# Differential attention heads: outputs normed into one kept tile and transposed together, first softmax left unnormalised

## The chip, the cores and the metric

The kernel runs on one core of a Trainium2 chip. The metric is device time in microseconds (us) of one execution, the median of three runs. A profiled execution gives the trace; its own time stands beside its span below.

## What is computed

Two blocks in sequence on 512 tokens of width 1024. The first block has two hybrid layers, each with 4 differential, 8 stick-breaking and 8 forgetting attention heads, an output projection and norms; the second block has a recurrent branch, windowed attention and a feed-forward part. The change touches only the differential heads of the two hybrid layers:

```python
def diff_attention(q, k, v, lam, lambda_init, sub_gain):
    ...
        s = jnp.einsum('bhcqd,bhckd->bhcqk', q[:, :, :, q0:q1], k[:, :, :, :q1]).astype(jnp.float32) * scale
        allowed = chunk_id[:q1][None, :] <= chunk_id[q0:q1][:, None]
        p = jax.nn.softmax(jnp.where(allowed, s, -jnp.inf), axis=-1)
        w = p[:, :, 0] - lam * p[:, :, 1]
        outs.append(jnp.einsum('bhqk,bhkd->bhqd', w, v[:, :, :q1].astype(jnp.float32)))
    o = jnp.concatenate(outs, axis=2)
    return rms_norm(o, sub_gain) * (1.0 - lambda_init)
```

Two softmaxes per head (`p[:, :, 0]`, `p[:, :, 1]`) are combined into one weight matrix `w`, multiplied with the values, and each output row of 128 is divided by its root mean square (with 1e-6 added to the mean square).

## The kernel before

All matrix products with weights are three TensorE passes over a high and a low part of each operand (`mm3`), so TensorE has most of the work. A layer is a stream of projections, chunk by chunk, into which the attention of the heads is woven. `Pipe` (line 316) holds the stages of attention steps with lags: a differential head has four query blocks (steps i = 0 to 3, of key width 128, 256, 384 and 512), each step has the stages `a`, `b_`, `c`, `d`, due 0, 3, 5 and 8 ticks after its start, two ticks to a step. In a tick the due stages are issued, the latest stage first but `a` last, and then `Filler` issues projection matmuls up to a share of its total. Differential heads are n = 0 to 3, pair heads (stick-breaking, forgetting) n = 4 to 11. Heads 0 and 1 are given 3 chunks of projections, the later ones 3.97.

A differential step before the change (line 695):

- `a`: scores of the two softmaxes on TensorE into two PSUM banks; per softmax VectorE masks a corner (L704) and finds the row maximum (L706), ScalarE takes the exponential and sums the row (L709), VectorE inverts the sum (L711). VectorE then multiplies the second inverse by minus lambda (L715), scales the first exponential by its inverse (L716) and adds the second one times its factor (L717, called the merge here).
- `b_`: TensorE transposes the merged weights by 128-blocks into a bank (L143), and VectorE or ScalarE in turn copies them out (L511 on VectorE, L513 on ScalarE).
- `c`: TensorE multiplies them with the values into a bank; ScalarE squares and sums (L730); `rstd_of` makes mean and power, a [128, 1] VectorE operation (L357) and a GpSimd power (L361); VectorE scales the output into one of two small tiles (L732).
- `d`: TensorE transposes that tile into a quarter of a bank that the head keeps from i = 0 to i = 3; at i = 3 VectorE multiplies with gain and gate (L741), and `split` makes high and low parts (L267 on ScalarE, L268 on GpSimd).

Beside it, `rope` rotates q and k of the next head: shuffle (L520) on VectorE, a product on GpSimd (L522), a product (L523) and a sum (L524) on VectorE, then splits (L618 on ScalarE, L619 on VectorE). Weights are split by L219 (ScalarE) and L233 (VectorE and GpSimd), the gate is L631 and L632.

A scheduler sets the order on VectorE, ScalarE and GpSimd and which buffer a tile gets; TensorE keeps program order (`tc.keep_in_program_order`). Buffers: 8 PSUM banks, 6 tiles of tag `wT`, 24 [128, 1] tiles of tag `st`.

## Time and profile before

| | |
|---|---|
| median of 3 runs | 1808.55 us (1807.75 to 1809.88) |
| profiled execution: its own time, its span | 1806.02 us, 1804.2 us |
| TensorE busy | 1760.4 us, 98% of the span |
| VectorE busy | 1125.7 us, 62% |
| ScalarE busy | 765.3 us, 42% |
| GpSimd busy | 646.0 us, 36% |
| mean granted clock of TensorE | 0.994 |

The span is 1.8 us shorter than the execution's own time. Busy time of TensorE includes time at a lower granted clock, since a slower matmul is still busy. The differential heads lie at about 60 to 206 us (first layer) and 500 to 640 us (second layer). All rows name engines as PE (TensorE), PEld (its weight loads), DVE (VectorE), ACT (ScalarE), POOL (GpSimd).

### The profile page before, as it was taken

To read this page: it belongs to the slowest core of one execution; us is meant where nothing else is said; L and a number is where in the kernel's file an instruction comes from. 1 tells how busy PE (TensorE), PEld (TensorE's weight loads), DVE (VectorE), ACT (ScalarE), POOL (GpSimd) and SP (SyncE) were. 2 spreads that over 40 slices of the span, in tenths; PEclk is the share of its full clock that TensorE was granted. 3 is DMA by queue.
4 is the path that set the end of the run, shared out by engine and by line. 5 is a ranking of instruction groups with operands and counts; after the bars stand their busy time and mean duration, and the time that the engine had idled before them with its cause. 6 is when DMAs were issued, how large, how long until landed. Compare 5 with 4: busy or idle time off the path is not lost.

```text
span 1804.2 us, 26056 instructions
## 1 busy us (share of the span) xinstructions
PE 1760.4 (98%) x9774; PEld 1516.4 (84%) x9774; DVE 1125.7 (62%) x2450; ACT 765.3 (42%) x1461; POOL 646.0 (36%) x534
## 2 busy tenths in 40 slices
PE   9989999999999999999999999999999999999998
PEld 8778887888978888888899888788788888888898
DVE  5788889775588899876583678886423632222122
ACT  4445444443445544444433433777423432322221
POOL 3332221122333222122253545355545344444331
PEclk9999999999999999999999999999999999999999
DMA  5312222312321312322223232222333233333321
GB/s 199 92 54 82 66 66 94 106 60 82 121 70 53 94 60 71 112 78 93 66 94 106 82 90 87 88 70 100 111 96 109 94 95 103 96 94 99 100 97 67
DMA packets 51696, 162.12 MB, mean 90 GB/s; under 512 B 8482, under 2 KB 10050, under 8 KB 51571
## 3 DMA queue, kind: packets, MB, share of 16 engines
q1 hardware_dynamic: 51570, 160.46, 28.1%
q8 instruction: 77, 1.26, 0.3%
q14 instruction: 49, 0.39, 0.1%
HBM read 158.28 MB, written 2.16 MB: 89 GB/s over the span
## 4 chain that ended last, share of the span: by engine, by line
PE 81%; DVE 10%; issue 3%; ACT 2%; POOL 2%; DMA 1%; SPq 0%; POOLq 0%; DVEq 0%; ACTq 0%
PE ps L126 78%; PE ps L143 3%; DVE wl L233 2%; POOL e L522 1%; DVE e L763 1%; DMA raw<-in_wu_dram 1%; DVE e L520 1%; DVE st L706 1%; POOL st L361 1%; DVE yT L523 0%; ACT wh L219 0%; POOL wl L233 0%; DMA x<-in_x_dram 0%; DVE klow L619 0%; DVE e L764 0%
## 5 line engine op out<-in xcount | busy, mean ns | idle before, releaser
L233 POOL TENSOR_TENSOR wl<-raw,wh 128x368 fp32r<-128x368 f32 (+5 forms) x262 | 359.3, 1373 | 634.6 <-ACT wh L219 587.5
L126 PE MATMUL ps<-hTH,wh 128*128 128x512 f32 (+1 forms) x1336 | 531.8, 398 | 1.4 <-DVE sm L1135 1.4
L126 PE MATMUL ps<-hTL,wh 128*128 128x512 f32 (+1 forms) x1336 | 521.8, 391 | 0.0
L126 PE MATMUL ps<-hTH,wl 128*128 128x512 f32 (+1 forms) x1336 | 521.8, 391 | 0.0
L219 ACT CAST wh<-raw 128x1024 fp32r<-128x1024 f32 (+2 forms) x263 | 269.1, 1026 | 403.2 <-PE ps L126 219.5
L233 DVE TENSOR_TENSOR wl<-raw,wh 128x656 fp32r<-128x656 f32 (+6 forms) x261 | 256.1, 982 | 283.7 <-ACT wh L219 282.0
L126 PEld LDWEIGHTS ps<-hTH,wl 128*128 128x128 f32 x1336 | 252.4, 189 | 53.8
L126 PEld LDWEIGHTS ps<-hTH,wh 128*128 128x128 f32 x1336 | 252.7, 189 | 49.4 <-issue 1.9
L126 PEld LDWEIGHTS ps<-hTL,wh 128*128 128x128 f32 x1336 | 252.9, 189 | 46.8
L126 PE MATMUL ps<-wh,yT 128*128 128x512 f32 (+1 forms) x544 | 161.5, 369 | 0.0
L126 PEld LDWEIGHTS ps<-wh,yT 128*128 128x128 f32 x544 | 98.5, 189 | 16.0 <-issue 0.3
L126 PE MATMUL ps<-wh,hTH 128*128 128x256 f32 (+2 forms) x496 | 106.5, 303 | 3.2 <-ACT hTH L383 1.7
L361 POOL TENSOR_TENSOR st<-st,half_neg 128x1 f32<-128x1 f32 x64 | 37.6, 587 | 198.3 <-DVE st L359 116.6
L126 PE MATMUL ps<-wl,hTH 128*128 128x256 f32 (+2 forms) x496 | 106.8, 300 | 0.5 <-POOL wl L233 0.5
L126 PE MATMUL ps<-wh,hTL 128*128 128x256 f32 (+2 forms) x496 | 105.7, 300 | 0.0
L126 PE MATMUL ps<-wl,yT 128*128 128x512 f32 (+1 forms) x272 | 99.4, 365 | 0.0
L126 PEld LDWEIGHTS ps<-wh,hTH 128*128 128x128 f32 x496 | 84.9, 208 | 5.0 <-ACT hTH L383 2.1
L143 PE MATMUL ps<-ident,e 128*128 128x128 f32 x460 | 71.1, 276 | 15.1 <-DVE e L764 5.8
L126 PEld LDWEIGHTS ps<-wl,hTH 128*128 128x128 f32 x496 | 84.6, 208 | 0.9 <-POOL wl L233 0.7
L126 PEld LDWEIGHTS ps<-wh,hTL 128*128 128x128 f32 x496 | 84.2, 208 | 0.1
L126 PE MATMUL ps<-y,y 128*128 128x128 f32 (+2 forms) x240 | 69.8, 322 | 6.1 <-ACT e L709 5.0
L143 PEld LDWEIGHTS ps<-ident,e 128*128 128x128 f32 x460 | 53.5, 141 | 26.0 <-issue 11.1
(331 smaller groups left out, 2851.2 us busy)
## 6 DMA issues: line engine op xcount, KB each, us to landing
raw<-in_wu_dram SPq DMA_DIRECT2D x263, 512.0 KB, 3.5
bc<-cum SPq DMA_DIRECT2D x16, 256.0 KB, 5.4
raw<-in_wu_dram SPq DMA_DIRECT2D x10, 256.0 KB, 2.5
yT<-back SPq DMA_DIRECT2D x8, 256.0 KB, 4.3
raw<-in_wu_dram SPq DMA_DIRECT2D x4, 396.0 KB, 3.0
x<-in_x_dram SPq DMA_DIRECT2D x3, 512.0 KB, 8.0
out_dram<-x SPq DMA_DIRECT2D x3, 512.0 KB, 2.7
gain<-in_post_norm_dram SPq DMA_DIRECT2D x2, 512.0 KB, 4.8
```

The costliest lines, as they stand in the source:

```text
L126: tc.keep_in_program_order(nc.tensor.matmul(*args, **kw))
L143: tc.keep_in_program_order(nc.tensor.transpose(dst, src, ident))
L219: order(copy(h[:, : r.shape[1]], r))
L233: order(e.tensor_tensor(lo[:, d], r[:, d], h[:, d].bitcast(F32), op=ALU.subtract))
L361: order(G.tensor_tensor(r, m, half_neg, op=ALU.pow))
L520: V.stream_shuffle(sh[:n], t[:n], mask)
L522: G.tensor_tensor(shv, shv, sinT, op=ALU.mult)
L706: V.tensor_reduce(mx, ps[:, :w], axis=AX.X, op=ALU.max, negate=True)
L763: V.tensor_tensor_scan(rev, rev, rev, 1.0, ALU.mult, ALU.bypass)
```

## The change

The first softmax is left unnormalised: the merged matrix is exp0 - lam * (sum0/sum1) * exp1, that is, w times the row sum of the first exponential. The norm that follows divides the scale out again; so that the 1e-6 has the right weight, it is multiplied by that row sum squared (`eps`) and added to the mean square. The normed outputs of the four steps go to the four quarters of one `wT` tile that the head keeps, and stage `d` does nothing until i = 3, where it takes a bank, transposes all four quarters into it and goes on as before.

```diff
             def a():
-                es, rs = [], []
+                es, dens = [], []
...
                     ACT.activation(e[:, :w], ps[:, :w], AF.Exp, bias=mx, accum_out=den)
-                    r = stat()
-                    V.reciprocal(r, den)
                     es.append(e)
-                    rs.append(r)
-                r1 = stat()
-                V.tensor_tensor(r1, rs[1], neglam, op=ALU.mult)
-                V.tensor_scalar(es[0][:, :w], es[0][:, :w], rs[0], None, ALU.mult)
+                    dens.append(den)
+                r1, eps = stat(), stat()
+                V.reciprocal(r1, dens[1])
+                V.scalar_tensor_tensor(r1, r1, neglam, dens[0], ALU.mult, ALU.mult)
                 V.scalar_tensor_tensor(es[0][:, :w], es[1][:, :w], r1, es[0][:, :w], ALU.mult, ALU.add)
-                loc["w"] = es[0]
+                V.scalar_tensor_tensor(eps, dens[0], EPS, dens[0], ALU.mult, ALU.mult)
+                loc["w"], loc["eps"] = es[0], eps
...
-                o1 = small(P, 2, "o1")
+                if i == 0:
+                    s["o1"] = [oall[:, P * q : P * (q + 1)] for oall in (work("wT"),) for q in range(4)]
+                o1 = s["o1"][i]
                 ssq = stat()
                 ACT.activation(o1, o[:, :P], AF.Square, accum_out=ssq)
-                r = rstd_of(ssq, P)
+                m, r = stat(), stat()
+                V.scalar_tensor_tensor(m, ssq, 1.0 / P, loc["eps"], ALU.mult, ALU.add)
+                G.tensor_tensor(r, m, half_neg, op=ALU.pow)
                 V.tensor_scalar(o1, o[:, :P], r, None, ALU.mult)
-                loc["o1"] = o1
 
             def d():
-                if i == 0:
-                    s["yps"] = bank()
-                transpose(s["yps"][:, P * i : P * (i + 1)], loc["o1"])
-                if i == 3:
-                    sg = s["sg"]
-                    V.scalar_tensor_tensor(sg, s["yps"], subl, sg, ALU.mult, ALU.mult)
-                    chunks[n] = split(sg, "yT")
+                if i < 3:
+                    return
+                yps = bank()
+                for q, o1 in enumerate(s["o1"]):
+                    transpose(yps[:, P * q : P * (q + 1)], o1)
+                sg = s["sg"]
+                V.scalar_tensor_tensor(sg, yps, subl, sg, ALU.mult, ALU.mult)
+                chunks[n] = split(sg, "yT")
```

In the changed kernel the lines of a step are: inverse L713, factor L714, merge L715, eps L716, square L731, mean L733, power L734, scaling of the output L735, gain and gate L744. Per step VectorE has one wide operation less (L716 of before) and as many [128, 1] operations as before (four). TensorE's order is the same but for the transposes of `d`; the DMA queue's order is the same.

The scheduler sets VectorE's and ScalarE's orders anew over all differential heads. VectorE, first layer, head 1, step 0 (128 wide): from the first row maximum to the merge. `ps_910`, `ps_911` (before) and `ps_899`, `ps_900` (changed) are the two score banks; `e_939` and `e_926` are the shuffled k or q of the next head.

Before:

```order
L706 TENSOR_REDUCE st_917<-ps_910 128x1
L732 TENSOR_SCALAR sm_885<-ps_882,st_890 128x128
L711 RECIPROCAL st_922<-st_920 128x1
L706 TENSOR_REDUCE st_925<-ps_911 128x1
L716 TENSOR_SCALAR e_919<-e_919,st_922 128x128
L511 COPY wT_982<-ps_977 128x512
L711 RECIPROCAL st_930<-st_928 128x1
L520 STREAM_SHUFFLE e_939<-e_937 128x512
L715 TENSOR_TENSOR st_932<-st_930,sm_477 128x1
L523 TENSOR_TENSOR e_937<-e_937,rope_464 128x512
L717 SCALAR_TENSOR_TENSOR e_919<-e_927,st_932,e_919 128x128
```

Changed:

```order
L706 TENSOR_REDUCE st_906<-ps_899 128x1
L704 MEMSET ps_900 64x64
L233 TENSOR_TENSOR wl_1234<-raw_1231,wh_1233 128x656
L706 TENSOR_REDUCE st_912<-ps_900 128x1
L713 RECIPROCAL st_917<-st_915 128x1
L716 SCALAR_TENSOR_TENSOR st_918<-st_909 128x1
L714 SCALAR_TENSOR_TENSOR st_917<-st_917,sm_477,st_909 128x1
L715 SCALAR_TENSOR_TENSOR e_908<-e_914,st_917,e_908 128x128
L520 STREAM_SHUFFLE e_926<-e_924 128x512
```

The inverse of the second sum now stands directly behind the second row maximum, with no other VectorE work between them; before, the wide scaling L716 and a PSUM copy stood there. The merge moved ahead of the shuffle.

ScalarE, first layer, head 0, steps 1 and 2: the copy (L513, 128x256) of step 1's transposed weights.

Before:

```order
L709 ACTIVATE e_797,st_798<-ps_781,st_795 128x384
L513 COPY wT_828<-ps_825 128x256
L631 ACTIVATE sg_830<-ps_760 128x512
L730 ACTIVATE sm_817,st_818<-ps_815 128x128
L709 ACTIVATE e_856,st_857<-ps_847,st_854 128x512
```

Changed:

```order
L709 ACTIVATE e_785,st_786<-ps_776,st_783 128x384
L631 ACTIVATE sg_824<-ps_756 128x512
L219 CAST wh_1115<-raw_1113 128x1024
L709 ACTIVATE e_791,st_792<-ps_777,st_789 128x384
L731 ACTIVATE wT_811,st_812<-ps_809 128x128
L513 COPY wT_822<-ps_819 128x256
L709 ACTIVATE e_850,st_851<-ps_841,st_848 128x512
```

The copy now stands behind the gate, a weight cast, step 2's second exponential and step 0's square; before, it stood directly behind step 2's second exponential, ahead of the gate and the square.

TensorE, first layer, stage `d` of head 0 at i = 3, just ahead of the scores of head 1, step 3.

Before:

```order
L143 MATMUL ps_908<-ident_84,sm_1056 128x128
L126 MATMUL ps_1154<-y_739,y_643 128x512
L126 MATMUL ps_1154<-klow_91,y_643 128x512
L126 MATMUL ps_1155<-y_739,y_643 128x512
L126 MATMUL ps_1155<-klow_91,y_643 128x512
```

Changed:

```order
L143 MATMUL ps_1127<-ident_84,wT_811 128x128 x4
L126 MATMUL ps_1137<-y_735,y_643 128x512
L126 MATMUL ps_1137<-klow_91,y_643 128x512
L126 MATMUL ps_1138<-y_735,y_643 128x512
L126 MATMUL ps_1138<-klow_91,y_643 128x512
```

Three transposes came here from earlier places. As placed in the built programs, the second score bank here (`ps_1155`, `ps_1138`) is in both kernels the bank of the first scores of the step before it (head 1, step 2), which that step's first exponential frees. The next value projection's second bank follows the output of a step in the kernel before (freed by L732), and an older tile, the transposed weights of head 2, step 0, in the changed one.

## Rows read from the trace of the kernel before

**Rows 1.** Busy us by stretch: PE, PEld, DVE, ACT, POOL; granted clock; DMA share, GB/s.
```profile
60.00:140.00 80.00, 71.90 (x380) 59.85 (x379) 70.08 (x179) 39.79 (x101) 27.66 (x26) 0.98 0.20 61
...
500.00:580.00 80.00, 73.41 (x393) 61.95 (x392) 67.59 (x182) 39.33 (x101) 27.89 (x26) 0.96 0.23 70
```

**Rows 2.** TensorE's timeline: start, us, instruction, [idle before <- what ended it].
```profile
104.03 0.33 PE L143 MATMUL ps<-ident,sm 128*128 128x128 f32 x1 [0.83 <-DVE sm L732]
...
107.25 0.50 PE L126 MATMUL ps<-y,y 128*128 128x512 f32 x1 [2.43 <-ACT e L709]
...
134.12 0.74 PE L126 MATMUL ps<-wh,hTH 128*128 128x256 f32 x4 [1.23 <-DVE sm L732]
...
519.63 0.52 PE L143 MATMUL ps<-ident,e 128*128 128x128 f32 x3 [2.54 <-DVE st L357]
...
544.22 0.50 PE L126 MATMUL ps<-y,y 128*128 128x512 f32 x1 [1.80 <-ACT e L709]
...
571.02 0.74 PE L126 MATMUL ps<-wh,hTH 128*128 128x256 f32 x4 [0.29 <-DVE sm L732]
```

**Rows 3.** VectorE's waits, 60 to 140 us: the two longest.
```profile
DVE sm L732 <- POOL st L361: 4.0, 6, 1.7
DVE st L711 <- ACT e L709: 2.0, 7, 0.4
```

**Rows 4.** VectorE's waits, 500 to 580 us: three of them.
```profile
DVE sm L732 <- POOL st L361: 5.2, 8, 1.7
DVE st L711 <- ACT e L709: 2.1, 4, 0.8
...
DVE ps L704 <- PE ps L126: 1.3, 1, 1.3
```

**Rows 5.** Line 716 alone (wide scaling) by stretch: DVE busy (count), clock, DMA.
```profile
60.00:140.00 80.00, 4.66 (x11) 0.98 0.20 61
...
500.00:580.00 80.00, 4.64 (x11) 0.96 0.23 70
```

**Rows 6.** Instructions of lines 715 and 359: ns min/median/max.
```profile
L715 DVE TENSOR_TENSOR st<-st,sm x32: 139/158/750, 70.0 to 608.9; 128x1 f32<-128x1 f32 x32
...
L359 DVE SCALAR_TENSOR_TENSOR st<-st,st,per_d x32: 210/219/533, 6.1 to 1798.9; 128x1 f32<-128x1 f32 x32
```

**Rows 7.** Groups by shape, 60 to 140 us: busy us, mean ns | idle before.
```profile
L511 DVE COPY wT<-ps 128x384 f32<-128x384 f32 x2 | 1.1, 548 | 0.0
...
L709 ACT ACTIVATION_READ_ACCUMULATOR e<-ps,st 128x1 f32 x22 | 4.2, 193 | 0.0
...
L709 ACT ACTIVATE e<-ps,st 128x256 f32<-128x256 f32 x6 | 2.8, 475 | 4.8 <-DVE st L706 4.8
L709 ACT ACTIVATE e<-ps,st 128x512 f32<-128x512 f32 x4 | 2.7, 687 | 4.7 <-DVE st L706 4.7
L709 ACT ACTIVATE e<-ps,st 128x128 f32<-128x128 f32 x6 | 2.2, 368 | 8.4 <-DVE st L706 8.4
```

**Rows 8.** Busy us in 2 us stretches, as rows 1: granted clock third from last.
```profile
108.00:110.00 2.00, 2.00 (x6) 1.50 (x6) 1.94 (x7) 1.76 (x6) 1.40 (x2) 0.50 0.00 0
110.00:112.00 2.00, 2.00 (x10) 1.65 (x9) 1.84 (x3) 0.60 (x1) 1.44 (x2) 0.66 0.33 61
...
546.00:548.00 2.00, 2.00 (x6) 1.61 (x5) 1.97 (x9) 1.33 (x5) 1.53 (x2) 0.50 0.00 0
```

**Rows 9.** VectorE's timeline after the differential heads: a wait for TensorE.
```profile
209.40 0.54 DVE L756 TENSOR_TENSOR ps<-ps,masks 128x128 f32<-128x128 f32 x2 [1.59 <-PE ps L126]
```

**Rows 10.** VectorE's timeline: two merges and two rotary products.
```profile
70.15 0.35 DVE L717 SCALAR_TENSOR_TENSOR e<-e,st,e 128x128 f32<-128x128 f32 x1
...
74.80 0.69 DVE L523 TENSOR_TENSOR e<-e,rope 128x512 f32<-128x512 f32 x1
...
92.50 1.38 DVE L717 SCALAR_TENSOR_TENSOR e<-e,st,e 128x128 f32<-128x128 f32 x1
...
130.69 1.78 DVE L523 TENSOR_TENSOR e<-e,rope 128x512 f32<-128x512 f32 x1
```

## The prediction

> **What bounds the kernel now.** I read the page first: TensorE is busy for 98% of the span, so only its idle time and its time at a low clock can be won. Then the busy time by stretch. While heads 0 and 1 run, TensorE is idle for 80 - 71.90 = 8.1 us in the first layer and 80 - 73.41 = 6.6 us in the second, and VectorE is busy for 70.1 and 67.6 of the 80 us [rows 1]. Together that is 14.7 us of idle time in the two stretches that the change can reach. In the waits view VectorE waits for GpSimd's power (4.0 and 5.2 us) and for the exponentials (2.0 and 2.1 us), and for TensorE only once, 1.3 us in the second layer [rows 3, 4]. So in these stretches VectorE's chain sets the pace: what comes off it comes off TensorE's idle time, up to the 14.7 us. The timeline of TensorE shows where it stands still [rows 2]: for merged weights (2.54 us at 519.63), for the normed output at i = 3 (0.83 us at 104.03), for a score bank that the last step's exponential must free (2.43 and 1.80 us at 107.25 and 544.22), and for a bank of the value projection (1.23 and 0.29 us at 134.12 and 571.02). After the longer ones the clock falls to its lower level: the granted clock is 0.50 and 0.66 in the two stretches of 2 us after 108 us, and 0.50 again at 546 us [rows 8]. The first costs (1 - 0.50) x 2 + (1 - 0.66) x 2 = 1.7 us.
>
> A gain here lasts. At 209.40 us VectorE waits 1.59 us for TensorE [rows 9]: from there VectorE has time over, and TensorE's earlier arrival is passed on.
>
> **Part by part.** *The wide scaling goes.* L716 takes 4.66 and 4.64 us in the two stretches, 11 runs each [rows 5]: 9.3 us off VectorE. The other 10 runs lie in heads 2 and 3, where TensorE has no idle time to win, and count nothing.
>
> *The [128, 1] operations stay four to a step, but three become scalar_tensor_tensor.* L715 takes 158 ns as a tensor_tensor, a scalar_tensor_tensor of this size 219 ns [rows 6]. That bounds the cost between 0 (the two that take constants run like L715) and 3 x 0.06 us a step. I take 0.10, since only the factor reads a scalar from memory as L359 does: 22 steps, 2.2 us.
>
> *VectorE has less to do while the second exponential runs.* In the order of head 1, step 0, the inverse now stands directly behind the second row maximum. It waits for an exponential and its read: 0.37 + 0.19 = 0.56 us at width 128, 0.67 at 256, 0.88 at 512 [rows 7]; 384 has no row here, and 0.78 lies between. Where a PSUM copy covers it (0.55 us at 384) 0.33 is left. Of the 11 steps of the stretch in the first layer six are bare or thinly covered: 2 x 0.56 + 0.67 + 0.5 + 2 x 0.4 = 3.1 us. In the second layer five are: 1.1 + 0.88 + 0.56 + 0.67 + 0.5 = 3.7 us (the 1.1 where the first exponential is late too). The sum is 6.8 us, against 4.1 us of such waits now [rows 3, 4]: 2.7 us more. Ends: 0, if the queues drift so that the exponential is done, and 6.8.
>
> *Waits for the power.* Between mean (L733) and scaling of the output (L735) less work stands than before: the gate product (L632) no longer stands there in the first layer. Going through the 11 steps of the first layer with about 0.7 us to cover, I find 3.6 us uncovered where the same count for the order before gives 2.5. I take 1.0 us a layer, 2.0 in all; ends 0 and 9.2, the waits there now [rows 3, 4], once more.
>
> *Transposes and banks.* There are 32 transposes of normed outputs before and after; three of four move to the last step of the head, so they cost TensorE nothing. The wait at 104.03 is for the fourth output and stays [rows 2]. The head's bank is free between i = 0 and i = 3, but taken just ahead of the scores at which TensorE waits at 107.25 and 544.22, and the second of these score banks still is that of the step before: the 2.43 and 1.80 us go only as far as VectorE gets faster. The value projection's bank comes from an older tile now: 1.23 + 0.29 = 1.5 us go [rows 2].
>
> *One kept `wT` tile.* In differential heads one or two of six are in use, so this costs nothing; a pair head needs all six, but takes the last two three ticks after the last differential head has given its tile back.
>
> *The clock.* If the stops at 107 and 544 us get shorter, the low clock behind them may stay away: 0 to 2 x 1.7 = 3.4 us, the second taken like the first [rows 8]. I take half, 1.7.
>
> **Sum.** VectorE's chain: 9.3 - 2.2 - 2.7 - 2.0 = 2.4 us; bank 1.5; clock 1.7; together 5.6 us. The profiled execution's own 1806.02 us becomes 1800.4. The median of the runs is 2.5 us above it, so for a median I take 1808.55 - 5.6 = 1803.0 us.
>
> **The rivals.**
>
> *Full relief.* The scheduler covers the new waits with weight splits, and only the dearer small operations are paid: 9.3 - 2.2 + 1.5 + 3.4 = 12.0 us, 1796.5 us. For it speaks that both exponentials can now follow the scores without an inverse between them, so banks come free earlier. Against it, the bare places in the order. Its limit is all idle time and both low stretches, 14.7 + 3.4 = 18.1 us.
>
> *The waits take it all.* If the wait for the exponential counts in full (6.8 instead of 2.7), VectorE's chain is 9.3 - 2.2 - 6.8 - 2.0 = -1.7 us, and without help from the clock 1.5 us of bank are left: about 1808.7, no change.
>
> *GpSimd blocks the merge.* In five places (head 0, step 1, and head 1, step 1, of both layers, and head 1, step 0, of the second) the merge now stands between the shuffle and the rotary product, as GpSimd starts its own product. A merge took 0.35 us at 70.15 and 1.38 us, at the same width, at 92.50 beside GpSimd's product; a rotary product took 0.69 us at 74.80 and 1.78 us at 130.69, behind a merge placed so [rows 10]. At five places 1.78 - 0.69 = 1.1 us each, 5.5 us: 1803.0 + 5.5 = 1808.5, no change. It decides only if GpSimd gets in between. The Trainium skill states it as a rule (SBUF — State Buffer, "SBUF: two separate sides"): a VectorE instruction with two SBUF inputs and a GpSimd instruction exclude each other, and the later one waits for the whole of the first. The two rows agree with that rule.
>
> *Slower: the copy of step 1 comes late.* ScalarE's copy of step 1's transposed weights (second layer: VectorE's) now stands behind the gate, a weight cast and the next step's second exponential. TensorE's value product needs it and would stop for up to a cast, a gate and an exponential more, some 2.5 us, at a place where it now has 1 to 2 us to wait anyway. If that costs 1.3 us a layer, a stop of this length also brings the low clock (1.7 us), and the stop at 107 us remains: 2 x 3.0 - 1.5 = 4.5 us, 1813.0 us. It decides from the point where the copy lands after the merged weights of step 2. Against it: the second exponential follows the first sooner now.
>
> **How the numbers follow.** About 0.2% (3.6 us) is what a measurement of this kernel can tell from no change: faster is below 1804.9, slower above 1812.2. The forecast has 0.45, of which 0.40 is below 1804.9; full relief 0.17; no change by the waits 0.21; by GpSimd 0.07; slower 0.10. So faster 0.40 + 0.17 = 0.57, same 0.05 + 0.21 + 0.07 = 0.33, slower 0.10. The range goes from a little below full relief, 1796.0, to 1809.5, a little above no change; it leaves out the slower case and half of what lies beyond full relief. The forecast's own range is 1800 to 1806.
>
> **What would show it.** Right: L716's wide operation is gone, TensorE's idle time from 60 to 140 and from 500 to 580 us sums to some 10 us instead of 14.7, the idle row on the value projection is gone, the wait of the inverse for the exponentials rises to about 7 us, and the stop at the fourth step's scores is below 2 us. Wrong: idle time in these stretches unchanged or higher, a stop at the value product of step 1, or low clock at a new place; or a gain that is lost again before 300 us, with new idle rows at the pair heads' transposes.

## The result and the profile after

The changed kernel takes 1817.44 us (median of 5 runs, 1816.39 to 1822.31); the kernel before took 1809.06 us beside it (5 runs, 1807.75 to 1811.68). The ratio is 1.0053, with a 95% interval from 1.0042 to 1.0065: 0.5% slower, where 0.3% faster was forecast. (The ratios here compare runs made side by side; they are not the quotients of the medians, which would be 1.0046.) The profiled execution took 1822.31 us, the slowest of the five, and the one of the kernel before, 1806.02 us, was faster than its other runs. So the two traces lie 16.3 us apart where the medians lie 8.4 us apart: where the time went can be read from them, the sums are too large.

Busy time by stretch, changed kernel, columns as in [rows 1]:

```profile
60.00:140.00 80.00, 68.93 (x365) 57.20 (x364) 67.60 (x163) 38.24 (x96) 27.31 (x25) 0.99 0.19 60
...
500.00:580.00 80.00, 73.07 (x380) 61.29 (x378) 65.18 (x160) 38.70 (x94) 28.70 (x26) 0.98 0.23 70
580.00:640.00 60.00, 56.79 (x312) 49.76 (x313) 46.48 (x120) 33.58 (x79) 19.20 (x19) 0.94 0.22 71
```

VectorE has less to do than before (67.60 and 65.18 us in the two stretches, against 70.08 and 67.59 in [rows 1]), and yet TensorE is busy for less of the first stretch (68.93 us against 71.90). In the second layer part of the new idle time lies after 580 us (60.00 - 56.79 = 3.2 us up to 640, where there was none). TensorE's timeline of the changed kernel shows where it stands still now; columns as in [rows 2]:

```profile
71.56 0.33 PE L143 MATMUL ps<-ident,e 128*128 128x128 f32 x1 [2.46 <-DVE e L715]
...
106.54 0.50 PE L126 MATMUL ps<-y,y 128*128 128x512 f32 x1 [1.05 <-ACT e L709]
...
138.49 0.50 PE L126 MATMUL ps<-y,y 128*128 128x512 f32 x1 [3.08 <-ACT e L709]
140.53 0.79 PE L126 MATMUL ps<-y,y 128*128 128x512 f32 x1 [1.17 <-ACT e L709]
...
515.63 0.33 PE L143 MATMUL ps<-ident,e 128*128 128x128 f32 x1 [2.69 <-DVE e L715]
527.32 0.68 PE L126 MATMUL ps<-V,wT 128*128 128x128 f32 x4 [1.74 <-DVE st L714]
...
551.21 0.50 PE L126 MATMUL ps<-y,y 128*128 128x512 f32 x1 [1.05 <-ACT e L709]
...
582.91 0.79 PE L126 MATMUL ps<-y,y 128*128 128x512 f32 x1 [2.96 <-ACT e L709]
584.43 0.80 PE L126 MATMUL ps<-y,y 128*128 128x512 f32 x1 [0.30 <-ACT e L709]
```

And the places in the kernel before that answer to the longest of them:

```profile
70.55 0.33 PE L143 MATMUL ps<-ident,e 128*128 128x128 f32 x1 [1.38 <-DVE e L717]
...
138.02 0.50 PE L126 MATMUL ps<-y,y 128*128 128x512 f32 x1 [0.20 <-ACT e L709]
...
506.70 0.33 PE L143 MATMUL ps<-ident,e 128*128 128x128 f32 x1 [0.20 <-DVE e L717]
...
574.94 0.50 PE L126 MATMUL ps<-y,y 128*128 128x512 f32 x1 [0.20 <-ACT e L709]
```

What the prediction wanted gone is gone or shorter: 2.43 and 1.80 us at the fourth step's scores of head 1 [rows 2] became 1.05 and 1.05, and no row waits for the value projection's bank any more. But a new stop has come before the scores of head 2, step 3: 3.08 + 1.17 us in the first layer and 2.96 + 0.30 us in the second, where there were 0.20 us each. The stop at the first merge of head 0 grew (2.46 and 2.69 us; before, 1.38 and 0.20 us). With the idle rows of 0.2 us and more added up, 60 to 146 and 500 to 590 us, TensorE stands still for 11.5 + 10.1 = 21.6 us instead of 8.1 + 6.6 = 14.7 us.

The clock follows. Stretches of 2 us, changed kernel, granted clock third from last:

```profile
108.00:110.00 2.00, 1.75 (x10) 1.35 (x8) 2.00 (x5) 0.84 (x5) 0.49 (x1) 1.00 0.00 0
...
138.00:140.00 2.00, 0.87 (x2) 0.30 (x2) 1.91 (x3) 0.63 (x3) 0.55 (x1) 0.74 0.00 0
140.00:142.00 2.00, 1.47 (x5) 1.28 (x6) 1.11 (x5) 1.16 (x6) 0.27 (x1) 0.50 0.78 213
142.00:144.00 2.00, 2.00 (x11) 2.00 (x11) 1.69 (x6) 0.71 (x2) 0.28 (x1) 0.50 0.16 61
144.00:146.00 2.00, 2.00 (x12) 2.00 (x12) 0.96 (x2) 1.38 (x4) 1.28 (x1) 0.56 0.00 0
```

The low clock behind 107 us [rows 8] has gone, as hoped, and stands behind the new stop instead, for longer: (0.26 + 0.50 + 0.50 + 0.44) x 2 = 3.4 us against 1.7. Over the profiled executions the balance is: span 1820.5 - 1804.2 = 16.3 us more. TensorE is busy 1768.5 - 1760.4 = 8.1 us longer, about what the low clock takes (1 minus the granted clock, summed over all 2 us stretches, rises from 10.1 to 17.9 us), and idle 8.2 us longer. In the two head stretches lie 21.6 - 14.7 = 6.9 us of the idle time and 8.5 - 5.1 = 3.4 us of the low clock, 10.3 us together. The other 4.4 us of low clock lie elsewhere, most of them at about 304, 747 and 1300 us.

### The profile page after: what moved, and what is told of

Read it like the earlier page. It is cut to its first block, busy times and chain, and to the rows that moved or that the text cites. A ratio compares the mean times of both kernels' runs of the same rounds, so it can differ in the third digit from the quotient of the medians.

```text
span 1820.5 us, 26031 instructions
## 1 busy us (share of the span) xinstructions
PE 1768.5 (97%) x9774; PEld 1523.8 (84%) x9774; DVE 1121.4 (62%) x2418; ACT 764.7 (42%) x1461; POOL 650.2 (36%) x534
## 4 chain that ended last, share of the span: by engine, by line
PE 78%; DVE 12%; ACT 3%; issue 3%; POOL 2%; DMA 2%; SPq 0%; POOLq 0%; DVEq 0%; ACTq 0%
PE ps L126 74%; PE ps L143 3%; DVE wl L233 2%; DMA raw<-in_wu_dram 1%; ACT wh L219 1%; DVE e L766 1%; DVE e L520 1%; POOL wl L233 1%; DVE yT L523 0%; POOL e L522 0%; POOL st L734 0%; DVE wT L511 0%; ACT y L618 0%; DVE st L706 0%; DVE e L524 0%
## 5 line engine op out<-in xcount | busy, mean ns | idle before, releaser
L233 POOL TENSOR_TENSOR wl<-raw,wh 128x368 fp32r<-128x368 f32 (+5 forms) x262 | 364.8, 1394 | 669.2 <-ACT wh L219 629.9
L233 DVE TENSOR_TENSOR wl<-raw,wh 128x656 fp32r<-128x656 f32 (+6 forms) x261 | 252.6, 969 | 290.1 <-ACT wh L219 288.1
L268 POOL TENSOR_TENSOR yT<-sg,yT 128x512 fp32r<-128x512 f32 x28 | 36.2, 1292 | 97.1 <-ACT yT L267 97.1
```

Of the source, the lines that this page charges most:

```text
L233: order(e.tensor_tensor(lo[:, d], r[:, d], h[:, d].bitcast(F32), op=ALU.subtract))
L268: G.tensor_tensor(lo, y, h.bitcast(F32), op=ALU.subtract)
```

## The experiments

Each run has its own runs of the kernel before beside it; the ratios are to those. "Stops" is TensorE's idle time in the two head stretches, as added up above, from one profiled execution of each (not added up for the three runs that stop beyond these stretches too). The changed kernel itself was run beside the kernel before only in the first row, 5 times each, and the median of the kernel before moves by 1.9 us between the rows; so a step from that row to another is given in ratios and in medians.

| Run | Median us | Before us | Ratio, 95% interval | Stops us |
|---|---|---|---|---|
| changed kernel | 1817.44 | 1809.06 | 1.0053 (1.0042 to 1.0065) | 21.6 |
| softmax part alone | 1816.83 | 1810.95 | 1.0032 (1.0020 to 1.0044) | 20.5 |
| together part alone | 1813.75 | 1810.95 | 1.0016 (1.0007 to 1.0025) | 17.4 |
| changed, sum first | 1817.59 | 1810.95 | 1.0038 (1.0023 to 1.0052) | 19.9 |
| changed, sum and merge first | 1814.40 | 1810.95 | 1.0027 (1.0016 to 1.0039) | 17.8 |
| changed, low split behind | 1813.00 | 1810.59 | 1.0015 (1.0005 to 1.0025) | 17.3 |
| changed, three orders | 1811.13 | 1810.59 | 1.0002 (0.9994 to 1.0011) | 15.0 |
| changed, four orders | 1811.79 | 1810.59 | 1.0011 (1.0002 to 1.0020) | 17.4 |
| before, four orders | 1807.00 | 1810.59 | 0.9989 (0.9980 to 0.9999) | 14.9 |
| changed, splits held back | 1861.62 | 1809.18 | 1.0287 (1.0263 to 1.0311) | |
| the same, merge before shuffle | 1863.83 | 1809.18 | 1.0290 (1.0267 to 1.0313) | |
| before, the same and the gate's order | 1892.48 | 1809.18 | 1.0452 (1.0433 to 1.0471) | |
| three orders, merge before shuffle | 1810.96 | 1810.29 | 1.0005 (0.9995 to 1.0016) | 16.9 |
| softmax part, three orders | 1808.73 | 1810.29 | 0.9989 (0.9980 to 0.9998) | 13.8 |
| together part, three orders | 1809.88 | 1810.29 | 0.9995 (0.9985 to 1.0005) | 14.6 |
| before, three orders | 1807.88 | 1810.29 | 0.9991 (0.9983 to 1.0000) | 14.6 |

### The parts alone, and the first theory

**Softmax part alone.** The changed kernel with the transposes of before:

```diff
-                if i == 0:
-                    s["o1"] = [oall[:, P * q : P * (q + 1)] for oall in (work("wT"),) for q in range(4)]
-                o1 = s["o1"][i]
+                o1 = small(P, 2, "o1")
```

(and stage `d` as before the change).

> Edit: the unnormalised first softmax alone; each step's normed output goes to its small tile and is transposed in its own step into the kept bank, as in the kernel before. My theory (T1): the loss of 8.4 us comes from VectorE's order, which the change as a whole happened to set: in the first rotation of the step before the stop, the scaling of the output (L735), which waits for GpSimd's power behind GpSimd's rotary product, stands ahead of the rotary sum (L524); all behind it, the casts of q and the exponential that frees the score bank, comes late (stops of 3.08 + 1.17 us at 138.49 and 2.96 + 0.30 us at 582.91 where before had 0.20 each). In this kernel the sum stands ahead of the scaling there, so by T1 these two stops stay below 1 us; the merge of head 0, step 0 still stands behind the next step's row maximum (2.46 and 2.69 us of stop there instead of 1.38 and 0.20). Time by T1: 1806 to 1812 us. Rival T3 (the kept tile and the late transposes cost it, by banks): this kernel is faster than before, 1800 to 1805. Rival T4 (the three dearer [128, 1] operations and the waits for exponentials in the softmax part cost it, whatever the order): 1815 to 1819, with stops spread over the heads.

**Together part alone.** The kernel before with the kept tile and the late transposes (the same lines the other way round, and stage `d` of the change).

> Edit: the kept tile and the transposing together alone, with the two softmaxes normalised as in the kernel before. In this kernel's order the rotary sum stands ahead of the scaling at head 2, step 1, and the first merge ahead of the next step's row maximum, as before. T1 (VectorE's order is the cause): stops at head 2, step 3 below 1 us, time like before, 1806 to 1811 us. T3 (kept tile, banks): 1814 to 1819, with the new stops at head 2, step 3. T4 (softmax part): like before, 1806 to 1811; this run does not tell T1 from T4, the first one does.

Neither is free: 1.0032 and 1.0016. The softmax part alone loses as T4 said, with its stops spread over the heads (for instance 1.49 us at 134.44 and 1.33 us at 139.65). But the new stop before head 2, step 3 appears in the together part as well, at 2.09 us, and that part's time is above what T1 and T4 allowed. So no one of the three theories holds as written for both runs.

**Changed, sum first.**

```diff
-        V.tensor_tensor(t[:n], t[:n], sh[:n], op=ALU.add)
+        sums.append(V.tensor_tensor(t[:n], t[:n], sh[:n], op=ALU.add))
...
-                V.tensor_scalar(o1, o[:, :P], r, None, ALU.mult)
+                behind(V.tensor_scalar(o1, o[:, :P], r, None, ALU.mult), sums)
```

`behind(ins, list)` here and below only tells the scheduler that `ins` comes after the list's last instruction on the same engine.

> Edit: the changed kernel with one order added on VectorE alone: the scaling of the output (L735) stands behind the last rotary sum (L524) issued in the program. Only two pairs of instructions per layer change places (head 1, step 0 and head 2, step 1); nothing is added or left out. T1: the stops of 3.08 + 1.17 us and 2.96 + 0.30 us before the scores of head 2, step 3 fall below 1 us each, and the low clock behind them (138 to 146 and 582 to 590 us, 3.4 us lost each in the profiled execution) goes or shrinks: 6 to 12 us faster than the changed kernel, 1805 to 1811 us. T3 and T4: no effect, 1815 to 1819 us.

Measured 1.0038. The stop shrank and stayed: 2.31 + 1.32 us (at 135.83 and 137.88) instead of 4.25, so in the first layer the wait for the power ahead of the sum was about a seventh of it. The median is that of the changed kernel (1817.59 against 1817.44 us). T1 falls as the main cause.

**Changed, sum and merge first.** As above, and

```diff
-                    V.tensor_reduce(mx, ps[:, :w], axis=AX.X, op=ALU.max, negate=True)
+                    behind(V.tensor_reduce(mx, ps[:, :w], axis=AX.X, op=ALU.max, negate=True), merges)
```

> Edit: as the run before, and on VectorE each step's row maxima behind the merge of the step before (one place per layer changes: the merge of head 0, step 0 comes ahead of step 1's first row maximum, as in the kernel before). T2: the stop at that merge (2.46 us at 71.56, 2.69 us at 515.63) shortens by about 1 us each, since the merge is then done before GpSimd's weight split begins (1.12 us for the merge beside it, 0.35 us alone in the kernel before): 1.5 to 3 us faster than the run before, 1802 to 1809 us, at or below the kernel before. If the merge is late for another reason: like the run before.

The stop at the first merge fell as expected, from 2.46 to 1.43 us and from 2.26 to 1.12 us, and the ratio by 0.0011, though the two intervals overlap. The median fell by 3.2 us, but to 1814.40 us, above the 1802 to 1809 expected. This order is a smaller part of the loss.

### The low split ahead of the row maximum

What was left showed in VectorE's timeline around head 2, step 2. Before the change:

```profile
132.58 0.69 DVE L524 TENSOR_TENSOR e<-e,e 128x512 f32<-128x512 f32 x1
...
134.22 0.56 DVE L706 TENSOR_REDUCE st<-ps 128x1 f32<-128x384 f32 x1
...
134.80 1.37 DVE L619 TENSOR_TENSOR klow<-e,y 64x512 fp32r<-64x512 f32 x2
```

After the change:

```profile
133.56 0.35 DVE L735 TENSOR_SCALAR wT<-ps,st 128x128 f32<-128x128 f32 x1 [1.69 <-POOL st L734]
133.83 0.68 DVE L524 TENSOR_TENSOR e<-e,e 128x512 f32<-128x512 f32 x1
135.19 1.39 DVE L619 TENSOR_TENSOR klow<-e,y 64x512 fp32r<-64x512 f32 x2 [0.69 <-ACT y L618]
...
137.17 0.56 DVE L706 TENSOR_REDUCE st<-ps 128x1 f32<-128x384 f32 x1
137.76 1.48 DVE L233 TENSOR_TENSOR wl<-raw,wh 128x656 fp32r<-128x656 f32 x1
```

Before, the row maximum (L706) came ahead of the low split (L619). Now VectorE first waits 0.69 us for ScalarE's cast, splits for 1.39 us, and only then takes the maximum; from the sum to the maximum it is 137.17 - 133.83 = 3.3 us instead of 1.6. ScalarE's timeline, before and then changed:

```profile
135.23 0.58 ACT L709 ACTIVATE e<-ps,st 128x384 f32<-128x384 f32 x1
```

```profile
137.76 0.58 ACT L709 ACTIVATE e<-ps,st 128x384 f32<-128x384 f32 x1 [0.26 <-DVE st L706]
...
139.80 0.58 ACT L709 ACTIVATE e<-ps,st 128x384 f32<-128x384 f32 x1 [1.37 <-DVE st L706]
```

The exponential starts at 137.76 us instead of 135.23, and it frees the score bank for which TensorE stands at 138.49. The step's second exponential, at 139.80, ends the second part of the stop (1.17 us at 140.53); it waits for the second row maximum, which in the changed kernel stands behind a weight split of 1.48 us (L233). Before, that split came behind both maxima. The low split stood ahead of the first maximum a step earlier too.

**Changed, low split behind.** The low split of the rotated q and k is issued to the scheduler behind the next step's first row maximum:

```diff
-                            V.tensor_tensor(lo, t[own], h.bitcast(F32), op=ALU.subtract)
+                            owed.append((n, lo, t[own], h.bitcast(F32)))
...
+                behind(V.tensor_tensor(o[1], o[2], o[3], op=ALU.subtract), rmaxes)
```

> After the first four runs T1 falls as the main cause: with the sum first, 2.31 + 1.32 us of 4.25 and 2.42 + 0.67 us of 3.26 stayed before the scores of head 2, step 3. New theory T5: in heads 2 and 3, where the prediction let VectorE count nothing, its order put the low split (L619, 1.4 us and a wait of 0.4 us for ScalarE's cast ahead of it) before the step's first row maximum (L706), at steps 1 and 2 of head 2; in the kernel before the row maximum came first at both. So each step's exponential, which frees the score bank, comes some 1.5 us later. Edit: the changed kernel; the low split is issued to the scheduler behind the next step's first row maximum and kept behind it, nothing else (the sum comes first at head 2, step 2, by itself). T5: the stops at head 2, step 3 fall to 0 to 1.5 us a layer, the low clock behind them goes, 4 to 9 us faster than the changed kernel, that is 0 to 5 us above the kernel before. If the [128, 1] operations and bare waits of the softmax part are the cause (T4): stops of 2.5 us or more stay, 6 to 9 us above the kernel before.

Measured 1.0015. VectorE and TensorE of this kernel (L726 is the maximum, L701 the low split):

```profile
131.91 0.55 DVE L726 TENSOR_REDUCE st<-ps 128x1 f32<-128x384 f32 x1
132.49 1.39 DVE L701 TENSOR_TENSOR klow<-e,y 64x512 fp32r<-64x512 f32 x2
```

```profile
136.69 0.50 PE L126 MATMUL ps<-y,y 128*128 128x512 f32 x1 [2.09 <-ACT e L729]
...
575.40 0.50 PE L126 MATMUL ps<-y,y 128*128 128x512 f32 x1 [0.89 <-ACT e L729]
```

The stop fell from 4.25 to 2.09 us and from 3.26 to 1.13 us (0.24 us at 573.78 with it), and the granted clock behind it is 1.00 from 138 to 142 and from 576 to 580 us. The ratio fell from 1.0053 to 1.0015, with intervals clear of each other, and the median by 4.4 of the 8.4 us: this edit takes away at least half of the loss. ScalarE's order from 60 to 146 us is the same in both traces. On VectorE the scheduler, given this order, also put the rotary sum ahead of the scaling and the merge behind the shuffle at head 2, step 1; the first of these is the order that gave little alone. The first layer's 2.09 us is above the 1.5 us that T5 allowed.

**Changed, three orders.** Sum first, merge first and low split behind, together.

> Edit: the changed kernel with three orders on VectorE: the rotary sum ahead of the scaling, the merge ahead of the next step's row maxima, the low split behind the step's first row maximum. If the three orders are what the change lost: the sum of what each gives, the stop at the merge of head 0, step 0 at 1.4 and below 1.2 us as in the run with the merge first, the stops at head 2, step 3 below 1.5 us: 3 to 6 us faster than with the low split alone, within 2 us of the kernel before or below it. By T4: 4 us or more above the kernel before.

Measured 1.0002: against the kernel before, the loss is gone, with stops of 15.0 us against 14.7. T4, by which 4 us or more should have stayed, falls. So the loss was, in the main, the order of VectorE's queue. But nothing is won. Two parts of the expectation missed: the step from the low split alone is 1.9 us in the medians, not 3 to 6, and a stop of 2.08 us stayed before head 2, step 3 in the first layer.

**Changed, four orders**, and **before, four orders**. The fourth keeps the gate behind the copies of transposed weights:

```diff
-                ACT.activation(sg, ps, AF.Tanh, scale=0.5)
-                V.scalar_tensor_tensor(sg, sg, 1.0, ps, ALU.add, ALU.mult)
+                behind(ACT.activation(sg, ps, AF.Tanh, scale=0.5), copies[1])
+                behind(V.scalar_tensor_tensor(sg, sg, 1.0, ps, ALU.add, ALU.mult), copies[0])
```

> Edit: as the run before, and the gate (L631 on ScalarE, L632 on VectorE) behind the last copy of transposed weights issued (L513, L511), so that the copy of step 1's weights of head 0 no longer waits behind the gate and a weight split. It tests my own slower case, in which that copy comes late: in the changed kernel TensorE stops for it 0.56 us at 82.08 and 1.74 us at 527.32. If the copy's place decides: these stops fall to 0.3 us or less, but the merged weights of step 2 come next on the same engine, so that half of it comes back there; 0.5 to 2 us faster than the run before, at or up to 4 us below the kernel before. If the copy is late for its input: no change.

> Edit: the kernel BEFORE the change with the same four orders. It tells what the orders are worth without the change. In the kernel before most of these orders hold already; the sum stands behind the scaling at head 1, step 1, where VectorE waits 1.68 us for the power ahead of the stop of 2.43 us at 107.25 (1.80 us at 544.22). Expected: 0 to 4 us faster than the kernel before. If the orders are worth as much here as in the changed kernel (6 us or more), the change itself gave nothing and lost nothing; if this run is like the kernel before and the run with four orders is faster, the change is worth that difference.

Of the stops for the copy of step 1, the first layer's fell (0.29 us instead of 0.79), the second layer's did not (1.97 us at 522.12), a stop of 2.26 us came at 542.55, and the time did not fall (1.0011). So this run tests the copy's place in the first layer only. The kernel before gains 0.1% from the same orders.

### What was missing between the row maxima and the inverse

**Changed, splits held back**, then **merge before shuffle**, and **before** with the same:

```diff
-                    order(e.tensor_tensor(lo[:, d], r[:, d], h[:, d].bitcast(F32), op=ALU.subtract))
+                    ins = order(e.tensor_tensor(lo[:, d], r[:, d], h[:, d].bitcast(F32), op=ALU.subtract))
+                    if e is V and ins is not None:
+                        behind(ins, rmaxes)
...
-        V.stream_shuffle(sh[:n], t[:n], mask)
+        behind(V.stream_shuffle(sh[:n], t[:n], mask), merges)
```

(the second piece only in the last two). All three hold the three orders as well. The last one holds the fourth, on the gate, too, which the first two do not.

> The run with three orders came to the kernel before (ratio 1.0002) and no lower, though VectorE has 4.1 us of wide scaling less per layer. Counted on VectorE from the first shuffle of head 1 (64.4 us) to the gain of head 1, the waits for exponentials are 2.55 us there (2.01 before) and the rotary products 7.85 us (5.60 before). Theory T6: the unnormalised softmax leaves nothing on VectorE between the second row maximum and the inverse, and the weight split (L233, 0.8 to 1.4 us), which could cover that wait, stands between the two row maxima, where it delays the second exponential. Edit: as the run with three orders, and each weight split on VectorE behind the last row maximum issued, so that it comes behind the second row maximum. T6: the inverse's waits for exponentials fall below 1 us per layer, the stop at head 2, step 3 (2.08 us and 1.15 us) below 1 us, 2 to 5 us faster than the run with three orders (0.997 to 0.999 of the kernel before). If these waits are off TensorE's path: like the run with three orders (0.9995 to 1.001).

> Edit: as the run before, and the rotary shuffle (L520) behind the merge (L715), so that the merge no longer stands between the shuffle and the rotary product while GpSimd runs its own rotary product. It tests the prediction's case in which GpSimd blocks VectorE: rotary products of 1.4 to 1.8 us should come down to 0.7 us in the places behind a merge (three or four per layer, some 1 us each on VectorE). If that reaches TensorE: 1 to 4 us faster than the run before. If the later shuffle gives it back (the rotation starts 0.5 us later): no change against the run before.

> Edit: the kernel BEFORE the change with the same orders as the run before this one (four orders of the earlier run of this kind, the weight split behind the row maximum, the shuffle behind the merge). It compares the change with its absence under like orders. If the change takes work off TensorE's path once VectorE's order is right, this run is 2 to 6 us slower than the run with the merge ahead of the shuffle. If VectorE's length no longer sets TensorE's pace, both are alike within 2 us. Against the kernel before I expect 0.997 to 0.9995.

All three missed by far. The weight splits are wanted at once; TensorE's timeline of the first one:

```profile
176.34 0.50 PE L126 MATMUL ps<-hTH,wl 128*128 128x512 f32 x1 [4.03 <-DVE wl L246]
```

Twelve such stops, 0.65 to 4.03 us each, stand in each layer's heads. The last two differ by 1892.48 - 1863.83 = 28.7 us, but they don't stand under like orders: the kernel before has the gate's order there and the changed kernel has not. How much of the 28.7 us is the change and how much that order, no run shows.

**Three orders, merge before shuffle.** The second piece of that diff alone, on the run with three orders.

> The two runs with the weight splits held back fell by 2.9%: TensorE stopped 1 to 4 us for each slab of split weights (rows on wl), so these splits are wanted at once and cannot serve as cover; nothing on the shuffle could be read there. Edit here: the run with three orders, plus the shuffle (L520) behind the merge (L715) alone; the weight splits stay where they were. If GpSimd's block of VectorE (rotary products of 1.78 us instead of 0.69 us, 2.2 us per layer) is on TensorE's path: 1 to 4 us faster than the run with three orders (0.998 to 0.9996 of the kernel before), with a stop before head 2, step 3 below the 2.08 us and 1.15 us there. If not: 0.9997 to 1.001.

Measured 1.0005. The rotary products of the first layer's heads, ns min/median/max: in the kernel before, with three orders, and here:

```profile
L523 DVE TENSOR_TENSOR e<-e,rope x6: 668/692/1782, 65.1 to 130.7; 128x512 f32<-128x512 f32 x6
```

```profile
L535 DVE TENSOR_TENSOR e<-e,rope x6: 683/1564/1785, 65.1 to 128.4; 128x512 f32<-128x512 f32 x6
```

```profile
L535 DVE TENSOR_TENSOR e<-e,rope x6: 682/692/1371, 65.1 to 129.0; 128x512 f32<-128x512 f32 x6
```

The long rotary products beside GpSimd's are real (median 1564 instead of 692 ns), most were taken away, and the time did not follow: TensorE's stops are 16.9 us in all, not below the 15.0 us of the run with three orders.

### The square

**Softmax part, together part and before, with the three orders each** (the edits of the parts and of the orders as in the diffs above):

> Edit: the unnormalised softmax alone (transposes step by step as before), with the three orders of VectorE. With the next two runs and the run with three orders it makes a square: neither part, each alone, both, all under like orders. If the loss of the softmax part (1.0032 when alone) was only order: 0.999 to 1.001. If the part itself costs by its waits for exponentials: 1.002 to 1.004 still.

> Edit: the kept tile and the transposing together alone (softmaxes normalised as before), with the three orders. If the loss of this part (1.0016 when alone) was order: 0.998 to 1.0. If the part itself costs (the bank of the late transposes, the output of step 3 waited for with three other transposes behind it): 1.001 to 1.003.

> Edit: the kernel before the change with the three orders (without the fourth, on the gate). Expected as with four: 0.998 to 1.0 of the kernel before. If it is faster than the changed kernel with the same orders (1.0002) by over 2 us, the change costs something of its own, apart from the order.

| | as the scheduler set them | three orders |
|---|---|---|
| neither part | 1 | 0.9991 |
| softmax part | 1.0032 | 0.9989 |
| together part | 1.0016 | 0.9995 |
| both | 1.0053 | 1.0002 |

Under like orders the four lie within 0.13% of each other, and their intervals overlap. Within that, the softmax part costs nothing and gives nothing (0.9989 against 0.9991). Both parts together stand 0.0011 above neither, 2.0 us by the ratios and 3.3 us by the medians; the last expectation set 2 us as the mark for a cost of the change's own. So by the ratios about four fifths of the loss are order (by the medians three fifths), and the rest may be the change itself, the kept tile beside the softmax part (1.0002 against 0.9989), which these runs don't settle. The fastest versions, the kernel before with four orders and the softmax part with three, beat the kernel before by 0.1%, which is below what counts here.

## Why the prediction was wrong

**The step that failed** is the reading on which the sum stands: "So in these stretches VectorE's chain sets the pace: what comes off it comes off TensorE's idle time". The sum's term for it, 2.4 us off VectorE's chain, was to be 2.4 us off TensorE's stops. It failed twice.

First, the scheduler's new order made the chain longer, and the sum had nothing for that. It counted the work and the waits of the steps, and put at nothing, without saying so, what a long split ahead of a row maximum costs. TensorE's new stops before head 2, step 3 are 7.5 us. Their place was not outside the count, as the expectation of the run with the low split has it: the 11 steps a layer are heads 0 and 1 and three steps of head 2. Line 716 of the kernel before, 60 to 140 us:

```profile
L716 DVE TENSOR_SCALAR e<-e,st x11: 275/345/1018, 67.7 to 137.2; 128x128 f32<-128x128 f32 x3, 128x256 f32<-128x256 f32 x3, 128x384 f32<-128x384 f32 x3, 128x512 f32<-128x512 f32 x2
```

Second, with the order held the chain did get shorter, and TensorE's idle time did not follow. From the first shuffle for head 1 to the gain of head 1, both layers added up (length, then busy time by engine), in the kernel before with three orders, in the changed kernel with three orders, and in that with the merge before the shuffle:

```profile
sum 152.88, PE 137.97 PEld 115.42 DVE 132.04 ACT 75.20 POOL 53.82; mean PE 68.99 PEld 57.71 DVE 66.02 ACT 37.60 POOL 26.91
```

```profile
sum 151.20, PE 136.10 PEld 113.66 DVE 130.92 ACT 74.20 POOL 52.22; mean PE 68.05 PEld 56.83 DVE 65.46 ACT 37.10 POOL 26.11
```

```profile
sum 150.73, PE 133.74 PEld 112.40 DVE 125.32 ACT 73.98 POOL 54.69; mean PE 66.87 PEld 56.20 DVE 62.66 ACT 36.99 POOL 27.35
```

The change makes these places 1.7 us shorter, near the 2.4 us of the sum, yet TensorE's stops are 15.0 us against 14.6. The later shuffle takes 5.6 us more off VectorE's busy time, and the places get 0.5 us shorter, with stops of 16.9 us. So in these runs the amount of VectorE's work does not set the pace; the order in which it hands on banks and weights does a part of it, and what else does stays open.

**VectorE's chain, term by term.** It was to get 2.4 us shorter. In the changed kernel as the scheduler ordered it, it got longer between the same two places in both layers (columns as [rows 1]; before, then changed):

```profile
64.30:140.65 76.35, 68.25 (x365) 56.90 (x364) 66.29 (x178) 37.36 (x97) 25.84 (x24) 0.98 0.21 64
...
500.44:577.76 77.32, 70.73 (x371) 59.36 (x370) 65.57 (x178) 37.70 (x96) 26.68 (x25) 0.96 0.22 66
```

```profile
64.23:142.78 78.55, 66.95 (x353) 55.72 (x352) 64.99 (x167) 37.26 (x97) 25.88 (x24) 0.98 0.20 66
...
508.28:586.65 78.37, 68.23 (x352) 56.91 (x351) 64.86 (x167) 37.63 (x96) 26.10 (x25) 0.95 0.23 71
```

76.35 to 78.55 and 77.32 to 78.37 us: 3.2 us longer (2.2 + 1.0), of which busy time is 2.0 us less and idle time 5.3 us more.

- *Less work.* The wide scaling is gone, 9.3 us. But VectorE's busy time fell by 1.3 + 0.7 = 2.0 us only, where 9.3 - 2.2 = 7.1 was expected. In the median the small operations are about 0.05 us a step dearer than before (L716 takes 141 ns, L714 219, L733 152), as priced or less. Added up, though, they take 18.9 us against 14.2, 4.7 us more instead of 2.2, since a few of them run long beside GpSimd's (last section). The rotary products take 14.4 us against 10.0, and the merges 13.0 against 16.9: GpSimd's products now lengthen the one instead of the other. In all, the durations sum to 4.4 us less; busy time, in which overlapping instructions count once, fell by less.
- *Waits for exponentials.* 2.7 us more expected; 3.2 + 3.6 against 2.0 + 2.1 [rows 3, 4] is 2.7 us (the changed kernel's over the stretches above). This term was right.
- *Waits for the power.* 2.0 us more expected; they fell a little (5.4 + 4.0 against 4.6 + 5.2 us in the same two stretches).
- *Waits that had no term.* VectorE's waits of the first layer's stretch in the changed kernel:

```profile
DVE wT L735 <- POOL st L734: 5.4, 8, 1.7
DVE st L713 <- ACT e L709: 3.2, 6, 0.7
DVE sg L632 <- ACT sg L631: 1.1, 2, 0.9
...
DVE klow L619 <- ACT y L618: 0.7, 1, 0.7
DVE y L619 <- ACT y L618: 0.7, 2, 0.4
DVE wl L233 <- ACT wh L219: 0.4, 1, 0.4
```

Before, the low split and the weight split did not wait here, and the gate for 0.2 us. The rows on L632, L619 and L233 sum to 2.9 us: in this order VectorE came to work that ScalarE had not prepared yet. That idle time grew in sum belongs to the order, not to the removed work: with three orders held in both, VectorE is idle between the same places for 152.88 - 132.04 = 20.8 us without the change and 151.20 - 130.92 = 20.3 us with it. Waits for ScalarE's preparation are longer there too, but waits for GpSimd and TensorE are shorter by as much.

**The bank of the value projection** was right: 1.23 + 0.29 us went. **The stops at 107 and 544 us** were right too: shorter, below 2 us, and their low clock went. **The clock** term had the wrong sign: in the head stretches the low clock took 8.5 us instead of 5.1, since the new stops brought more than the old ones took along.

**The rivals.** "Slower: the copy of step 1 comes late" had the right sign and a wrong place, so that this case, had it been chosen, would have been right by luck. The copy does come late (1.74 us at 527.32), but the kernel before stood 2.54 us at the next merge there [rows 2]; bringing the copy forward in the first layer won nothing. "GpSimd blocks the merge" names a thing that happens: the rotary products got 4.4 us longer, near the 5.5 us priced. But the merges got 3.9 us shorter, which that price left out, and taking the long products away gave no time. Of what the prediction listed as signs of being wrong, three came: idle time "unchanged or higher", "a stop at the value product of step 1" and "low clock at a new place".

**What stays open.** What sets TensorE's pace in these stretches beside the order, and whether the change itself costs the last 0.1%. The 2.08 us before head 2, step 3 that the changed kernel with three orders keeps in the first layer are a weight split (L245 there) between the two row maxima (L726, at 132.75 and 136.16 us); VectorE, then TensorE:

```profile
134.87 1.37 DVE L245 TENSOR_TENSOR wl<-raw,wh 128x656 fp32r<-128x656 f32 x1
136.16 0.55 DVE L726 TENSOR_REDUCE st<-ps 128x1 f32<-128x384 f32 x1
```

```profile
137.53 0.50 PE L126 MATMUL ps<-y,y 128*128 128x512 f32 x1 [2.08 <-ACT e L730]
```

The second exponential, which ends this stop, waits 2.15 us for the second maximum. The run that held the weight splits back held all of them, so no run shows what moving this one alone would give. The start of layer 2 varies too: the stop at its first merge was 1.12, 0.27 and 1.28 us in three kernels with the merge first.

## What to carry to other kernels

Where a scheduler sets the order, a change to one step is a change to all queues: compare the order at every place where an engine hands on a buffer, also where nothing is to be won, and look for long work with slack (here a split for a later head) that has slipped ahead of short work without slack (here a row maximum). To tell work from order, hold a few instructions in the old order in both kernels, the same ones in each; here that showed that most of the loss was order, and that the parts give nothing. And a busy engine is not yet the one that sets the pace: under like orders 9.3 us of wide work less left VectorE's chain 1.7 us shorter, and TensorE stood still as long as before.

## What the runs showed of the hardware

A [128, 1] operation can be held until GpSimd's next to it ends. The mean was a tensor_scalar with one input tile before (L357, 140 to 155 ns in all 32 steps); as a scalar_tensor_tensor with two inputs from SBUF it took up to 1.25 us. VectorE, then GpSimd, changed kernel:

```profile
121.83 1.25 DVE L733 SCALAR_TENSOR_TENSOR st<-st,st 128x1 f32<-128x1 f32 x1
```

```profile
121.27 1.79 POOL L522 TENSOR_TENSOR e<-e,rope 128x512 f32<-128x512 f32 x1 [2.97 <-DVE e L520]
```

Both end together, at 123.1 us. Six of the 64 new operations (L733 and L716) took over 0.8 us, each ending within 0.03 us of a GpSimd instruction, so this cost some 5 us of VectorE's time in all (an estimate: their 5.9 us less six times the median). The Trainium skill (SBUF — State Buffer, "SBUF: two separate sides") says that of a VectorE instruction with two SBUF inputs and a GpSimd instruction that reads SBUF, whichever starts first has their shared pair of ports for its whole length and the other is blocked; the two rows agree with that, and show that an operation on one column can be the one that is held.

The same stop does not always bring the low clock. Before the pair heads' transposes TensorE stands 1.06 and then 1.72 us in the changed kernel, and 1.04 and 1.72 us in the kernel before; the granted clock then fell to 0.50 from 304 to 306 us in the first and stayed at 1.00 from 298 to 302 us in the second. Each is one execution, so whether the kernel or the execution makes the difference is not shown. The spread of one kernel is of this size and more: 24 runs of the kernel before lay between 1806.35 and 1813.91 us.
